# Two-layer attention trunk: softmax weights as the stationary operand of the value matmuls of B, C and D

## The chip, the cores and the metric

One core of a Trainium2 chip runs the whole program. The metric is the device time of one execution in microseconds (us). The kernel before takes 2915.13 us, the median of three runs (2912.08 to 2920.03). In the profile, PE is TensorE's matmuls, PEld its weight loads, DVE VectorE, ACT ScalarE, POOL GpSimd and SP the engine that issues the DMAs.

## The reference

The input x is 2048 rows of 1024 values. Two layers, each with a residual:

```
z = rms_norm(x, ln_g) @ w_in                  # even layer: A and B; odd layer: C and D
q, k = rms_norm(q), rms_norm(k)               # per head of 64
s = q k^T / 8 + bias, masked;  p = softmax(s) # A: two softmaxes, w = p0 - lambda p1
o = p @ v                                     # heads of 64 (A: v of 128, o normed again)
x = x + concat(o * silu(gate)) @ w_out
```

B has 8 heads and sees all earlier rows, its bias is a cumulated forget gate. C has 8 query and 2 key/value heads in a window of two blocks of 128 rows, with a sink per head in the softmax's sum. D has 8 heads and sees up to five blocks, with a bias table by distance.

## The kernel before, in words

Everything runs in blocks of 128 rows (16 of them). Numbers are carried as f32r, a form of f32 that TensorE rounds; a factor that must not lose its rest is split into a high part h (f32r) and a low part l = value - h. The profile prints f32r as f32 in TensorE's rows.

The program is a list of steps, one per block and unit: 4 units of A (64 steps), 4 of B, 16 steps of output projection, 2 units of C, 4 of D, 16 steps of projection. Each step has pieces of four kinds: p (projection: 24 matmuls of 512 columns, `proj`, L214 to L216, then evacuation, norms, gate in `post`), t (transposes of q and k, L248), q (scores, L303, then a fused bias and running minimum on DVE, L306, and the exponential with its sum on ACT, L322) and v (weights times values). `drive` (L815) merges p of step i+2, q of step i and v of step i-1 by cost numbers that stand beside each piece; a scheduler behind it then places every instruction on its engine's in-order queue. A step's x (loads) runs up to four steps ahead.

The v piece of B, C and D is `pairs_av` (L332). It works on pairs of heads. A group of up to four weight tiles of 128 x 128 is transposed on TensorE (`ptp`, L344) into one PSUM bank, copied by ACT to h and by DVE to l (`ptb`, f32r, h and l side by side). Each tile is then one matmul (L365): V is the stationary operand, with its own 64 high and 64 low columns side by side, and h and l together are the moving operand of 256 columns. The result `OT` has head dimensions on its partitions, so it is already transposed; of its four quarters three are wanted, and `end` (L368) adds them with two ACT copies and four DVE operations. The gate is scaled by the softmax's reciprocal sums on DVE, transposed on TensorE (`ptg`, L355) and multiplied in. The product goes to DRAM transposed (`mixT`), and `out_proj` (L673) loads it and splits it on ACT and POOL without a transpose; only A's half of layer 0 is stored as rows (`mix`) and transposed in `out_proj` (`psm`, L689).

A's v (L449) works the other way: the transposed weights are the stationary operand. Per tile it has a matmul of h against V's 128 high and 128 low columns (`OA`, L479) and one of l in bf16 against a bf16 copy of V (L482).

PSUM holds two banks for z, two for scores (`pS`), three for transposes (`pT`) and one for outputs (`pO`).

Of the kernel before, what the change touches and what calls it, by code (L numbers as in the profile page):

```python
# [56 lines left out]
class Trunk:  # L57
    def __init__(self, ctx, tc, t):
# [35 lines left out]
        self.mix = dt_("mix", [P, DM // 2])  # L94
        self.mixT = [dt_("mixTa", [P, DM // 2]), dt_("mixTb", [P, DM])]
# [77 lines left out]
    def transposed(self, xs, dst):  # L173

        nc = self.nc
        for half, x in enumerate(xs):
            ps = self.pT.tile([P, 4, P], F32, tag="t", name="psx")
            for i in range(4):
                nc.tensor.transpose(ps[:, i], x[:, P * i:P * i + P], self.idf[:])  # L179
            xt = self.ap.tile([P, 4, 2, P], F32R, tag="pt", name="xnT", bufs=5)  # L180
            self.split(xt[:, :, 0], xt[:, :, 1], ps[:], nc.scalar, nc.vector)
            nc.sync.dma_start(dst[:, 1024 * half:1024 * half + 1024], xt[:].bitcast(F32).rearrange("p k a t -> p (k a t)"))
# [77 lines left out]
    def v_split(self, z):  # L260
# [5 lines left out]
        return V  # L266

    def silu2(self, z, mul=None):

        nc = self.nc  # L270
        g = self.ap.tile([P, P], F32, tag="gate", name="gate", bufs=8)
# [7 lines left out]
    def qk_row(self, row_st, q, ks, slot, kb0, m, bias, scale, recip):  # L279
# [12 lines left out]
        def piece(i, b, n):  # L292
# [18 lines left out]
            if i == len(cuts) - 1:  # L311
                self.exp_row(row_st, state["prev"], recip)
# [4 lines left out]
    def exp_row(self, row_st, nmax, recip):  # L317
        nc = self.nc
        s = self.sm.tile([P, 2], F32, tag="rs", name="rs")
# [3 lines left out]
        if len(rows) == 2:  # L323
            nc.vector.tensor_tensor(out=s[:, 0:1], in0=s[:, 0:1], in1=s[:, 1:2], op=ALU.add)
        row_st["s"] = s[:, 0:1]
        if recip is not None:
            nc.vector.reciprocal(s[:, 0:1], s[:, 0:1])
            if recip != 1.0:
                nc.gpsimd.tensor_scalar(out=s[:, 0:1], in0=s[:, 0:1], scalar1=recip, scalar2=1.0, op0=ALU.mult, op1=ALU.mult)


    def pairs_av(self, pairs):  # L332
# [3 lines left out]
        groups = [(pr, pr["items"][i:i + 4]) for pr in pairs for i in range(0, len(pr["items"]), 4)]  # L336
        hls = {}

        def tr(gi):
            g = groups[gi][1]  # L340
# [4 lines left out]
            hl = hls[gi] = ap.tile([P, 4, 2, P], F32R, tag="pt", name="ptb", bufs=5)  # L345
            self.split(hl[:, :n, 0, :], hl[:, :n, 1, :], pt[:, :n], nc.scalar, nc.vector)

        def gate(pr):

            g = pr["gate"]()  # L350
            for h in range(2):
                s = slice(64 * h, 64 * h + 64)
                nc.vector.tensor_scalar(out=g[:, s], in0=g[:, s], scalar1=pr["r"][h](), scalar2=0.5, op0=ALU.mult, op1=ALU.mult)
            pt = self.pT.tile([P, P], F32, tag="t", name="ptg")
            nc.tensor.transpose(pt[:], g[:], self.idf[:])  # L355
            gT = pr["gT"] = ap.tile([P, P], F32, tag="gT", name="gT", bufs=2)
            nc.scalar.activation(gT[:], pt[:], AF.Copy)

        def mm(gi):
            pr, g = groups[gi]  # L360
            if "OT" not in pr:
                pool, tag = (self.pO, "o") if pr is pairs[0] else (self.pS, "s")
                pr["OT"] = pool.tile([P, 2, 2, P], F32, tag=tag, name="OT")
            for i, (h, _, V, first, last) in enumerate(g):
                nc.tensor.matmul(pr["OT"][:, h].rearrange("p a b -> p (a b)"), V, hls[gi][:, i].rearrange("p a b -> p (a b)"),  # L365
                                 start=first, stop=last, skip_group_check=True)

        def end(pr):  # L368
            OT = pr["OT"]
            o = ap.tile([P, P], F32, tag="oT", name="oT", bufs=1)  # L370
            top, bot = slice(0, 64), slice(64, 128)
            nc.scalar.activation(o[top], OT[bot, 0, 0], AF.Copy)
            nc.scalar.activation(o[bot], OT[top, 1, 0], AF.Copy)
            nc.vector.tensor_tensor(out=o[top], in0=OT[top, 0, 0], in1=o[top], op=ALU.add)
            nc.vector.tensor_tensor(out=o[bot], in0=OT[bot, 1, 0], in1=o[bot], op=ALU.add)
            nc.vector.tensor_tensor(out=o[top], in0=OT[top, 0, 1], in1=o[top], op=ALU.add)
            nc.vector.tensor_tensor(out=o[bot], in0=OT[top, 1, 1], in1=o[bot], op=ALU.add)
            out = ap.tile([P, P], F32, tag="out", name="out", bufs=2)
            nc.vector.tensor_tensor(out=out[:], in0=o[:], in1=pr["gT"][:], op=ALU.mult)
            nc.sync.dma_start(pr["dst"], out[:])  # L380
        pieces = []
        n = len(groups)
        for gi in range(n + 1):
            if gi < n:
                pieces.append((0.107 * len(groups[gi][1]), lambda gi=gi: tr(gi)))
            if gi:
                pr, g = groups[gi - 1]
                pieces.append((0.107 * len(g), lambda gi=gi: mm(gi - 1)))
                if gi == n or groups[gi][0] is not pr:
                    pieces.append((0.107, lambda pr=pr: gate(pr)))  # L390
                    pieces.append((0.0, lambda pr=pr: end(pr)))
# [8 lines left out]
    def unit_A(self, h, W, X):  # L400
# [4 lines left out]
        def mk(tb):  # L405
# [3 lines left out]
            def p():  # L409
# [8 lines left out]
                def post():  # L418
# [8 lines left out]
                    Vb = self.bp.tile([P, P], BF16, tag="Vb", name="Vb", bufs=18)  # L427
# [14 lines left out]
            def q():  # L442
                st["r"] = [{}, {}]
                out = []
                for c in range(2):
                    out += self.qk_row(st["r"][c], lambda c=c: st["q"][c], ks, c, 0, m, bias, slope, 1.0 if c == 1 else None)
                return out

            def v():  # L449
# [3 lines left out]
                def tr(gi):  # L453
                    r0, r1 = st["r"]
                    j, cm = groups[gi]
                    if gi == 0:
                        cf = st["cf"] = self.sm.tile([P, 1], F32, tag="cf", name="cf")
                        nc.vector.tensor_scalar(out=cf[:], in0=r1["s"], scalar1=r0["s"], scalar2=self.nlam[:, 0:1], op0=ALU.mult, op1=ALU.mult)
# [11 lines left out]
                    l = self.bp.tile([P, 4, P], BF16, tag="ptl", name="ptl", bufs=3)  # L470
# [13 lines left out]
                def end():  # L484
                    O, gate = st["O"], st["gate"]
                    sq = ap.tile([P, P], F32, tag="oT", name="oT", bufs=1)
                    r0 = self.sm.tile([P, 2], F32, tag="r0", name="r0")
                    nc.vector.reciprocal(r0[:, 0:1], st["r"][0]["s"])
                    o = ap.tile([P, P], F32, tag="out", name="out", bufs=2)
                    nc.scalar.activation(o[:], O[:, 0], AF.Copy, scale=r0[:, 0:1])  # L490
                    nc.vector.scalar_tensor_tensor(out=o[:], in0=O[:, 1], scalar=r0[:, 0:1], in1=o[:], op0=ALU.mult, op1=ALU.add)
                    nc.scalar.activation(sq[:], o[:], AF.Square, accum_out=r0[:, 1:2])
                    y = self.rstd(r0[:, 1:2], 1, P, "x")
                    nc.vector.scalar_tensor_tensor(out=o[:], in0=o[:], scalar=y[:, 0:1], in1=gate[:], op0=ALU.mult, op1=ALU.mult)
                    nc.sync.dma_start(self.mix[tb][:, h * P:h * P + P], o[:])
# [12 lines left out]
    def unit_BD(self, kind, u, W, X):  # L508
# [15 lines left out]
        def mk(tb):  # L524
# [35 lines left out]
            def q():  # L560
                st["r"] = [{}, {}]
                out = []
                for h in range(2):
                    out += self.qk_row(st["r"][h], lambda h=h: st["q"][h], ks, h, kb0, m,
                                       lambda b, n, h=h: bias(h, b, n), 1.0, 1.0)
                return out

            def v():
                def w(h, j):
                    return lambda: st["r"][h]["rows"][j // 8][0][:, j % 8 * P:j % 8 * P + P]  # L570
                c0 = P * (u if kind == "B" else 4 + u)
                return self.pairs_av([dict(
                    items=[(h, w(h, j), vs[kb0 + j][:, h], j == 0, j == m - 1) for h in range(2) for j in range(m)],
                    r=[lambda h=h: st["r"][h]["s"] for h in range(2)], gate=lambda: st["gate"], dst=self.mixT[layer][tb][:, c0:c0 + P])])
# [18 lines left out]
    def unit_C(self, kv, W, Wkv, KV, X):  # L593
# [4 lines left out]
        def mk(tb):  # L598
# [6 lines left out]
            def p():  # L605
# [16 lines left out]
                def post():  # L622
# [3 lines left out]
                    st["gate"] = [self.silu2(z[:, 256 + P * i:384 + P * i]) for i in range(2)]  # L626
# [35 lines left out]
            def v():  # L662
                def w(g, j):
                    return lambda: st["row"][:, g, j * P:j * P + P]
                return self.pairs_av([dict(
                    items=[(h, w(2 * i + h, j), vs[kb0 + j][:, kv], j == 0, j == m - 1) for h in range(2) for j in range(m)],
                    r=[lambda g=2 * i + h: st["st"][:, g, 1:2] for h in range(2)], gate=lambda i=i: st["gate"][i],
                    dst=self.mixT[1][tb][:, (2 * kv + i) * P:(2 * kv + i + 1) * P]) for i in range(2)])
# [4 lines left out]
    def out_proj(self, layer, W, hook, done):  # L673
        nc = self.nc

        def mk(tb):
            st = {}

            def x():
# [4 lines left out]
                if layer == 0:  # L684
                    nc.sync.dma_start(mf[:, :512], self.mix[tb][:])
                    nc.sync.dma_start(mf[:, 512:], self.mixT[0][tb][:])
                    ps = self.pT.tile([P, 4, P], F32, tag="t", name="psm")
                    for i in range(4):
                        nc.tensor.transpose(ps[:, i], m[:, i], self.idf[:])  # L689
                else:  # L690
                    nc.sync.dma_start(mf, self.mixT[1][tb][:])
                for half, (h, l, _) in enumerate(st["x"]):
                    if layer == 0 and half == 0:
                        self.split(h, l, ps[:], nc.scalar, nc.vector)
                    else:
# [381 lines left out]
```

## Time and profile before

| | |
|---|---|
| median of three runs | 2915.13 us (2912.08 to 2920.03) |
| profiled execution | 2917.31 us |
| its span, first to last instruction | 2915.5 us |
| TensorE's mean granted clock | 0.989 of full speed |
| busy: PE, PEld | 2819.3, 2383.4 us |
| busy: DVE, ACT, POOL | 2187.9, 1920.4, 1249.3 us |
| A, to the end of its value matmuls | 60 to 815 us (the start takes 60) |
| B | 815 to 1587 us |
| first projection, C, D, last projection | to 1820, 2160, 2740, 2916 us |

Stages overlap at their borders, since the projection of the next unit runs beside the values of the last. Matmuls are pipelined: a matmul's duration in the profile contains latency that overlaps with its neighbours, so the distance between starts tells what it costs, and busy time does not. A weight load (PEld) of the next matmul runs beside the current one. "Idle before" in a group's row is the engine's idle time just ahead of its instructions, with what ended it.

### The profile page before, as it was taken

The page shows a single profiled execution, that of the slowest core. Times are in us where ns is not written, and L with a number is a line of the kernel's source. Part 1 is how long each engine was busy: PE and PEld are TensorE (multiplying, and loading weights), DVE is VectorE, ACT ScalarE, POOL GpSimd, SP SyncE. Part 2 cuts the span into 40 slices and gives each one's busy share as a digit, 9 for nine tenths or more (in the row PEclk, how much of TensorE's full clock was granted, in tenths as well). Part 3 has the DMA queues.
Part 4 walks back from the last instruction along what each step waited for, and adds up shares of the span by engine and source line. Part 5 has one row for each costly group of instructions (what it writes and reads, how often), then busy time and mean ns, then how long its engine had stood idle before and what let it go on. Part 6 is the DMA issues. An engine that isn't in the chain of part 4 may idle for free. (4 is left out here: it accounts for less than half of the span.)

```text
span 2915.5 us, 51639 instructions
## 1 busy us (share of the span) xinstructions
PE 2819.3 (97%) x16256; PEld 2383.4 (82%) x16256; DVE 2187.9 (75%) x7388; ACT 1920.4 (66%) x5127; POOL 1249.3 (43%) x1900
## 2 busy tenths in 40 slices
PE   7999999999999999999999999999999999999999
PEld 5778778787788888888878887988888888888887
DVE  6898887888888788788787334888987778777611
ACT  6567767677677677776776225878877776767510
POOL 5776565655644334333341113343233434343421
PEclk8999999999999999999999999999999999999999
DMA  8433433333333433423324555234443434343442
GB/s 293 157 129 128 134 121 123 107 111 110 115 103 100 131 100 103 143 90 128 116 67 154 216 195 181 98 115 147 137 145 124 154 127 145 126 156 116 148 152 94
DMA packets 159889, 389.30 MB, mean 134 GB/s; under 512 B 18144, under 2 KB 51936, under 8 KB 159616
## 3 DMA queue, kind: packets, MB, share of 16 engines
q1 hardware_dynamic: 159616, 386.00, 39.6%
q8 instruction: 130, 2.13, 0.3%
q14 instruction: 143, 1.17, 0.1%
HBM read 318.75 MB, written 67.17 MB: 132 GB/s over the span
## 5 line engine op out<-in xcount | busy, mean ns | idle before, releaser
L214 PE MATMUL z<-wh,x 128*128 128x512 f32 x1792 | 740.3, 414 | 20.0 <-DVE x L106 13.6
L216 PE MATMUL z<-wh,x 128*128 128x512 f32 x1792 | 715.8, 400 | 4.4 <-POOL x L108 3.6
L215 PE MATMUL z<-wl,x 128*128 128x512 f32 x1792 | 717.3, 400 | 0.8 <-DVE wl L154 0.8
L322 ACT ACTIVATE row<-row,mx 128x1024 f32<-128x1024 f32 (+7 forms) x512 | 440.8, 862 | 191.3 <-DVE mx L306 187.4
L303 PE MATMUL pss<-kT,qT 128*128 128x512 f32 (+3 forms) x1728 | 489.8, 369 | 27.7 <-DVE mx L306 26.1
L214 PEld LDWEIGHTS z<-wh,x 128*128 128x128 f32 x1792 | 342.1, 191 | 76.3 <-ACT wh L153 9.9
L216 PEld LDWEIGHTS z<-wh,x 128*128 128x128 f32 x1792 | 341.1, 190 | 74.3 <-POOL x L108 5.4
L215 PEld LDWEIGHTS z<-wl,x 128*128 128x128 f32 x1792 | 342.7, 191 | 53.3 <-DVE wl L154 3.1
L303 PEld LDWEIGHTS pss<-kT,qT 128*128 128x128 f32 x1728 | 295.2, 190 | 80.4 <-DVE mx L306 40.8
L108 DVE TENSOR_TENSOR ptb<-ptp,ptb 128x512 fp32r<-128x512 f32 (+1 forms) x520 | 326.9, 636 | 20.5 <-ACT ptb L104 16.6
L104 ACT ACTIVATE ptb<-ptp 128x512 fp32r<-128x512 f32 (+1 forms) x520 | 278.2, 554 | 79.9 <-PE ptp L344 73.5
L365 PE MATMUL OT<-ptb,V 128*128 128x256 f32 x1896 | 314.7, 292 | 12.3 <-DVE ptb L108 11.8
L365 PEld LDWEIGHTS OT<-ptb,V 128*128 128x128 f32 x1896 | 273.4, 191 | 43.9 <-DVE ptb L108 20.9
L116 POOL TENSOR_TENSOR y<-v,mhalf 128x4 f32<-128x4 f32 (+2 forms) x326 | 293.3, 901 | 19.7
L108 POOL TENSOR_TENSOR hl<-zs,hl 128x256 fp32r<-128x256 f32 (+1 forms) x240 | 174.0, 725 | 248.4 <-DVE hl L106 170.9
L344 PE MATMUL ptp<-idf,row 128*128 128x128 f32 x1648 | 258.3, 274 | 6.5 <-DVE ptb L108 5.2
L344 PEld LDWEIGHTS ptp<-idf,row 128*128 128x128 f32 x1648 | 198.2, 141 | 37.3 <-DVE ptb L108 4.0
L222 ACT ACTIVATE zs<-z,rs 128x512 f32<-128x512 f32 (+1 forms) x240 | 159.8, 667 | 88.2 <-PE z L216 83.3
L108 POOL TENSOR_TENSOR V<-zs,V 128x128 fp32r<-128x128 f32 x144 | 67.3, 469 | 274.4 <-ACT V L104 274.3
L108 POOL TENSOR_TENSOR wl<-wraw,wh 128x512 fp32r<-128x512 f32 x118 | 154.0, 1311 | 40.6 <-ACT wh L104 34.0
L714 DVE TENSOR_TENSOR res<-zo,res 128x512 f32<-128x512 f32 x64 | 44.0, 689 | 168.2 <-PE zo L216 166.8
L108 POOL TENSOR_TENSOR x<-mixr,x 128x512 fp32r<-128x512 f32 x48 | 62.1, 1296 | 249.8 <-ACT x L104 239.4
(186 smaller groups left out, 6069.3 us busy)
## 6 DMA issues: line engine op xcount, KB each, us to landing
x<-xs SPq DMA_DIRECT2D x416, 512.0 KB, 3.6
wraw<-in_w_dram SPq DMA_DIRECT2D x64, 256.0 KB, 2.8
xs<-x SPq DMA_DIRECT2D x32, 512.0 KB, 4.3
xs<-xnT SPq DMA_DIRECT2D x32, 512.0 KB, 3.3
xraw<-in_xT_dram SPq DMA_DIRECT2D x32, 256.0 KB, 4.2
x<-in_x_dram SPq DMA_DIRECT2D x32, 256.0 KB, 5.8
biasB<-cumd SPq DMA_DIRECT2D x32, 256.0 KB, 3.9
wraw<-in_wo_dram SPq DMA_DIRECT2D x32, 256.0 KB, 2.6
```

The source lines that it names most:

```text
L104: nc.scalar.activation(hi, src, AF.Copy)
L108: lo_eng.tensor_tensor(out=lo, in0=src, in1=h, op=ALU.subtract)
L116: nc.gpsimd.tensor_tensor(out=y[:], in0=v[:], in1=self.mhalf[:, :n], op=ALU.pow)
L214: nc.tensor.matmul(ps(), xh[:, i, :], wh, start=(kb == 0), stop=False)
L215: nc.tensor.matmul(ps(), xh[:, i, :], wl, start=False, stop=False)
L216: nc.tensor.matmul(ps(), xl[:, i, :], wh, start=False, stop=(kb == KB - 1))
L222: self.nc.scalar.activation(zs[:, :n], z[:, :n], AF.Copy, scale=self.rs[layer][:, tb:tb + 1])
L303: nc.tensor.matmul(ps[:, :w], q()[:, j, :], k[:, slot, (b % 4) * P:(b % 4) * P + w], start=(j == 0), stop=(j == 1))
L322: nc.scalar.activation(row[:, :hm * P], row[:, :hm * P], AF.Exp, scale=-1.0, bias=nmax, accum_out=s[:, i:i + 1])
L344: nc.tensor.transpose(pt[:, i], it[1](), self.idf[:])
L365: nc.tensor.matmul(pr["OT"][:, h].rearrange("p a b -> p (a b)"), V, hls[gi][:, i].rearrange("p a b -> p (a b)"), start=first, stop=last, s ...
L714: nc.vector.tensor_tensor(out=o[:, s], in0=st[n][:], in1=o[:, s], op=ALU.add)
```

## The change

`pairs_av` becomes `heads_av`. For B, C and D the transposed weights are now the stationary operand, as in A: per tile one matmul of h (f32r) against V's 64 high and 64 low columns (128 columns), and one of l (now bf16) against a bf16 copy of V's head (64 columns). The result has rows on its partitions; ACT and DVE add its two halves, DVE multiplies by the reciprocal sums and by the gate, for two heads at once in B and D and four in C. The gate isn't transposed any more. Rows go to DRAM as f32 in `mix`, and `out_proj` transposes all eight tiles of a block on TensorE, in both layers, and splits them on ACT and DVE. `v_split` makes the bf16 copy of V on ACT. In A and in the softmax's sums, sums and reciprocals of two rows are joined into one operation (`two_sums`, `add_sums`); `pt` tiles are half as large, with five `ptl` tiles (A had three), two `oT` tiles and an own pair of `xnT` tiles. The cost numbers of the v pieces change with it.

```
@@ v_split
-        return V
+        Vb = self.kvp.tile([P, 2, 64], BF16, tag="Vb", name="Vb", bufs=19)
+        nc.scalar.activation(Vb[:].rearrange("p h d -> p (h d)"), z, AF.Copy)
+        return V, Vb
...
+    def add_sums(self, st):
+        s = st["s"]
+        if len(st["r"][0]["rows"]) == 2:
+            self.nc.vector.tensor_tensor(out=s[:, :, 0], in0=s[:, :, 0], in1=s[:, :, 1], op=ALU.add)
...
-    def pairs_av(self, pairs):
+    def heads_av(self, nh, items, r, gate, dst):
...
-            hl = hls[gi] = ap.tile([P, 4, 2, P], F32R, tag="pt", name="ptb", bufs=5)
-            self.split(hl[:, :n, 0, :], hl[:, :n, 1, :], pt[:, :n], nc.scalar, nc.vector)
-
-        def gate(pr):
-
-            g = pr["gate"]()
-            for h in range(2):
-                s = slice(64 * h, 64 * h + 64)
-                nc.vector.tensor_scalar(out=g[:, s], in0=g[:, s], scalar1=pr["r"][h](), scalar2=0.5, op0=ALU.mult, op1=ALU.mult)
-            pt = self.pT.tile([P, P], F32, tag="t", name="ptg")
-            nc.tensor.transpose(pt[:], g[:], self.idf[:])
...
+            h = ap.tile([P, 4, P], F32R, tag="pt", name="pth", bufs=5)
+            l = ap.tile([P, 4, P], BF16, tag="ptl", name="ptl", bufs=5)
+            hls[gi] = h, l
+            self.split(h[:, :n], l[:, :n], pt[:, :n], nc.scalar, nc.vector)
 
         def mm(gi):
...
-            for i, (h, _, V, first, last) in enumerate(g):
-                nc.tensor.matmul(pr["OT"][:, h].rearrange("p a b -> p (a b)"), V, hls[gi][:, i].rearrange("p a b -> p (a b)"),
-                                 start=first, stop=last, skip_group_check=True)
...
+            for head in sorted({it[0] for _, it in g}):
+                own = [(i, it) for i, it in g if it[0] == head]
+                for i, (_, _, V, first, last) in own:
+                    nc.tensor.matmul(O[:, head], h[:, i], V[0], start=first, stop=False, skip_group_check=True)
+                for i, (_, _, V, first, last) in own:
+                    nc.tensor.matmul(O[:, head, 0:64], l[:, i], V[1], start=False, stop=last, skip_group_check=True)
+
+        def end():
+            O = st["O"]
+            o = ap.tile([P, nh, 64], F32, tag="oT", name="oT", bufs=2)
+            nc.scalar.activation(o[:], O[:, :, 64:128], AF.Copy, scale=0.5)
+            nc.vector.scalar_tensor_tensor(out=o[:], in0=O[:, :, 0:64], scalar=0.5, in1=o[:], op0=ALU.mult, op1=ALU.add)
+            nc.vector.tensor_tensor(out=o[:], in0=o[:], in1=r().unsqueeze(2).broadcast_to([P, nh, 64]), op=ALU.mult)
+            out = ap.tile([P, nh * 64], F32, tag="out", name="out", bufs=2)
+            nc.vector.tensor_tensor(out=out[:], in0=o[:].rearrange("p h d -> p (h d)"), in1=gate()[:], op=ALU.mult)
+            nc.sync.dma_start(dst, out[:])
...
-                pieces.append((0.107 * len(g), lambda gi=gi: mm(gi - 1)))
+                pieces.append((0.095 * len(groups[gi - 1]), lambda gi=gi: mm(gi - 1)))
...
@@ out_proj
-                if layer == 0:
-                    nc.sync.dma_start(mf[:, :512], self.mix[tb][:])
-                    nc.sync.dma_start(mf[:, 512:], self.mixT[0][tb][:])
+                nc.sync.dma_start(mf, self.mix[layer][tb][:])
+                for half, (h, l, _) in enumerate(st["x"]):
                     ps = self.pT.tile([P, 4, P], F32, tag="t", name="psm")
                     for i in range(4):
-                        nc.tensor.transpose(ps[:, i], m[:, i], self.idf[:])
...
-                        self.split(h, l, m[:, 4 * half:4 * half + 4], nc.scalar, nc.gpsimd)
+                        nc.tensor.transpose(ps[:, i], m[:, 4 * half + i], self.idf[:])
+                    self.split(h, l, ps[:], nc.scalar, nc.vector)
```

What this makes of the order shows at three places. The first is TensorE's queue in unit B, at a group of four weight tiles of one head; before (`row` holds the weights, `V` the values of one block, z is the projection of a later step):

```order
L215 MATMUL z_15592<-wl_11409,x_15258 128x512
L216 MATMUL z_15592<-wh_11408,x_15258 128x512
L344 MATMUL ptp_15301<-idf_87,row_15116 128x128 x4
L365 MATMUL OT_15165<-ptb_15178,V_14384 128x256
L365 MATMUL OT_15165<-ptb_15178,V_14514 128x256
L365 MATMUL OT_15165<-ptb_15178,V_14639 128x256
L365 MATMUL OT_15165<-ptb_15178,V_14769 128x256
```

and in the changed kernel, where `pth` is h and `ptl` is l (line numbers have shifted, so L213 to L215 are `proj` here):

```order
L214 MATMUL z_16967<-wl_14437,x_16469 128x512
L367 MATMUL OT_16545<-V_14530,pth_16603 128x128
L367 MATMUL OT_16545<-V_14651,pth_16603 128x128
L367 MATMUL OT_16545<-V_14786,pth_16603 128x128
L367 MATMUL OT_16545<-V_14929,pth_16603 128x128
L215 MATMUL z_16967<-wh_14436,x_16469 128x512
L213 MATMUL z_16967<-wh_14550,x_16469 128x512
L369 LDWEIGHTS ptl_16604
L369 MATMUL OT_16545<-Vb_14533,ptl_16604 128x64
```

Four matmuls became four with h and, here after two matmuls of a later projection, four with l, of which the first stands in the last two rows; each of them changes the stationary operand.

The second is DVE's queue in B, where a pair of heads ends; before:

```order
L374 TENSOR_TENSOR oT_21981<-OT_21861,oT_21981 64x128
L375 TENSOR_TENSOR oT_21981<-OT_21861,oT_21981 64x128
L106 CAST hl_22181<-zs_22159 128x4x64
L108 TENSOR_TENSOR ptb_22054<-ptp_22049,ptb_22054 128x4x128
L306 ISA row_22063,mx_22062<-pss_22083,biasB_20289,mx_22062 128x512
L306 ISA mx_22062 128x1
L376 TENSOR_TENSOR oT_21981<-OT_21861,oT_21981 64x128
L377 TENSOR_TENSOR oT_21981<-OT_21861,oT_21981 64x128
```

and in the changed kernel:

```order
L375 SCALAR_TENSOR_TENSOR oT_21454<-OT_21364,oT_21454 128x128
L376 TENSOR_TENSOR oT_21454<-oT_21454,rs_20978 128x128
L107 TENSOR_TENSOR ptl_21523<-ptp_21517,pth_21522 128x512
L378 TENSOR_TENSOR out_21458<-oT_21454,gate_20953 128x128
L308 ISA row_21496,mx_21470<-pss_21497,db_21500,mx_21470 128x128
```

Four additions of half tiles, spread over other work, became one of a whole tile, with two multiplications behind it.

The third is TensorE's queue in the last projection, at the border of two blocks (`zo` is the projection's PSUM tile, `mixr` the loaded rows); before:

```order
L214 MATMUL zo_39860<-wk_38813,x_39707 128x512
L215 MATMUL zo_39860<-wk_38813,x_39707 128x512
L216 MATMUL zo_39860<-wk_38813,x_39707 128x512
L214 MATMUL zo_39889<-wh_36789,x_39769 128x512
L215 MATMUL zo_39889<-wl_36790,x_39769 128x512
```

and in the changed kernel:

```order
L213 MATMUL zo_40106<-wk_39032,x_39915 128x512
L214 MATMUL zo_40106<-wk_39032,x_39915 128x512
L215 MATMUL zo_40106<-wk_39032,x_39915 128x512
L694 MATMUL psm_40137<-idf_87,mixr_40135 128x128 x4
L213 MATMUL zo_40153<-wh_36966,x_39987 128x512
```

Four transposes of a later block's rows stand between the matmuls, in a queue that held none of them in this layer.

More of the change, by code (lines that the diff above doesn't have):

```diff
@@ L368, in end @@
[L368 to L380, printed above, removed]
+            h = ap.tile([P, 4, P], F32R, tag="pt", name="pth", bufs=5)
@@ L625, in post @@
                     next(g)
-                    st["gate"] = [self.silu2(z[:, 256 + P * i:384 + P * i]) for i in range(2)]
+                    st["gate"] = self.silu2(z[:, 256:512])
                     next(g)
```

110 lines of the change are left out of this document (53 added, 57 removed).

## The prediction

> **What bounds the kernel now.** I read the page's busy shares first, then the stages (windows), then what TensorE waits for, and last its timeline, because a pipelined engine's busy time does not show what one of its instructions costs.
>
> ```profile
> span 2915.5 us, 51639 instructions
> PE 2819.3 (97%) x16256; PEld 2383.4 (82%) x16256; DVE 2187.9 (75%) x7388; ACT 1920.4 (66%) x5127; POOL 1249.3 (43%) x1900
> ```
>
> ```profile
> 60.00:815.00 755.00, 720.76 (x4258) 587.82 (x4258) 646.16 (x2047) 508.99 (x1360) 474.60 (x701) 0.99 0.37 123
> 815.00:1587.00 772.00, 757.30 (x4586) 653.00 (x4584) 638.83 (x2151) 563.79 (x1377) 289.36 (x477) 1.00 0.34 110
> 1587.00:1820.00 233.00, 228.11 (x1145) 189.83 (x1144) 91.44 (x247) 83.71 (x202) 51.19 (x83) 0.97 0.56 202
> 1820.00:2160.00 340.00, 328.54 (x2024) 287.55 (x2023) 290.07 (x1139) 281.19 (x888) 128.92 (x198) 0.98 0.40 129
> 2160.00:2740.00 580.00, 572.38 (x3330) 494.03 (x3329) 454.99 (x1630) 416.67 (x1140) 236.03 (x358) 0.99 0.41 134
> 2740.00:2916.00 176.00, 170.40 (x768) 140.77 (x766) 31.56 (x61) 24.30 (x48) 38.74 (x30) 1.00 0.38 134
> ```
>
> The six rows are A, B, the first output projection, C, D and the last projection; after the colon pair stand the length and the busy time of PE, PEld, DVE, ACT and POOL, then clock and DMA. TensorE is idle for 772.0 - 757.3 = 14.7 us in B, 11.5 in C and 7.6 in D, together 34 us of 1692, and for 34 us in A. DVE is at 83%, 85% and 78% in B, C and D. So TensorE sets the time in all the stages that change, and what remains idle there mostly waits for DVE:
>
> ```profile
> L365 PE MATMUL OT<-ptb,V 128*128 128x256 f32 x1896 | 314.7, 292 | 12.3 <-DVE ptb L108 11.8
> PE pss L303 <- DVE mx L306: 26.1, 39, 1.8
> ```
>
> The busy time of a row of matmuls overlaps with its neighbours', so costs have to come from start to start. One stretch of B, and the same stretch's weight loads (PEld):
>
> ```profile
> 1003.38 0.40 PE L216 MATMUL z<-wh,x 128*128 128x512 f32 x1
> 1003.61 0.63 PE L365 MATMUL OT<-ptb,V 128*128 128x256 f32 x4
> 1004.09 0.60 PE L344 MATMUL ptp<-idf,row 128*128 128x128 f32 x4
> ```
>
> ```profile
> 1003.99 0.46 PEld L344 LDWEIGHTS ptp<-idf,row 128*128 128x128 f32 x4
> 1004.41 0.54 PEld L365 LDWEIGHTS OT<-ptb,V 128*128 128x128 f32 x4
> ```
>
> A 512-column f32r matmul takes 1003.61 - 1003.38 = 0.23 us, a value matmul of 256 columns (1004.09 - 1003.61)/4 = 0.12 (its loads, 0.19 long by the mean below, start (0.54 - 0.19)/3 = 0.117 apart; I use 0.119). So 256 columns cost 0.11, and a 128-column f32r matmul would stream for about 0.12 - 0.055 = 0.065 us if columns alone counted. They do not:
>
> ```profile
> 1940.37 0.97 PEld L646 LDWEIGHTS psC<-kT,qT 128*128 128x128 f32 x8
> 1940.40 1.08 PE L646 MATMUL psC<-kT,qT 128*128 128x128 f32 x8
> 1941.32 0.62 PE L344 MATMUL ptp<-idf,rowC 128*128 128x128 f32 x4
> ```
>
> These eight matmuls of C's scores have an f32r operand of 128 columns and a new f32r stationary operand each, the form the change brings in. They take (1941.32 - 1940.40)/8 = 0.115 us apiece, not 0.065. The loads show why: one lasts 0.19 (its mean below), so eight in 0.97 start (0.97 - 0.19)/7 = 0.111 apart. The loads run one after the other; a matmul shorter than 0.111 us waits for the next load, a 256-column one (0.12) just hides it.
>
> **The change part by part.** *Value matmuls.* Removed: 1896 matmuls of 256 columns at 0.119: 225.6 us, their loads hidden. Added: 1896 matmuls h of 128 f32r columns and 1896 matmuls l of 64 bf16 columns, each with its own load. For l the nearest rows are A's bf16 matmuls of 128 columns:
>
> ```profile
> 511.40 0.40 PE L482 MATMUL OA<-Vb,ptl 128*128 128x128 bf16 x4
> 511.61 0.72 PE L479 MATMUL OA<-VA,pth 128*128 128x256 f32 x4
> ```
>
> ```profile
> L365 PEld LDWEIGHTS OT<-ptb,V 128*128 128x128 f32 x1896 | 273.4, 191 | 43.9 <-DVE ptb L108 20.9 <-ACT ptb L104 0.8 <-issue 0.7
> L344 PEld LDWEIGHTS ptp<-idf,row 128*128 128x128 f32 x1648 | 198.2, 141 | 37.3 <-DVE ptb L108 4.0 <-issue 3.7 <-PE pss L303 1.4
> L482 PEld LDWEIGHTS <-ptl 128*128 128x128 bf16 x544 | 31.7, 98 | 29.6 <-issue 9.8 <-DVE ptl L108 6.5 <-DVE mx L306 2.9
> ```
>
> Four take 511.61 - 511.40 = 0.21, or 0.052 each, for 128 columns. An f32r load of 191 ns occupies 111, so 80 of a load's duration is latency; then a bf16 load (98) occupies 18 ns and that of a transpose (141) 61. With 64 columns l lies between its load, 18 ns, and the 128-column row, 52; I take half the stream and a few ns, 30.
>
> What a load costs depends on the matmul ahead of it, so I counted neighbours in the built order of TensorE. Of the matmuls with f32r weights, 1362 stand behind an h (1193 of them h) and 515 behind an l (369 of them h); 186 transposes stand behind an l. The sum in us: streams 1896 x 0.065 = 123.2 and 1896 x 0.030 = 56.9; loads sticking out behind an h 1362 x (0.111 - 0.065) = 62.7, behind an l 515 x (0.111 - 0.030) = 41.7; transposes behind an l 186 x (0.061 - 0.030) = 5.8. Total 290.3, against 225.6: **+65 us**. Bounds: l at 18 or 52 ns moves only the 1195 l that follow an l, by -14 or +26; were h's own stream as long as its load, the 477 l and few others behind an h would add some 25. So +50 to +115.
>
> The Trainium skill, "TensorE: Matmul & The Clock Gate", section "Back-to-back issue gap", gives 81 ns per matmul in a stream of loads and matmuls of 128 columns; by it the 3792 new ones would take an estimated 307 us, +81, the same sign.
>
> *Transposes.* The 192 gate transposes go and 192 of mixed rows come (4 more per block of 128 rows in the first projection, 8 in the last), one kind of instruction at one price, by the loads of the stretch above (0.46 - 0.14)/3 = 0.107 each: 0 on TensorE in all, 21 us moved out of B, C and D, into the projections. There they stand in TensorE's queue behind a load from DRAM, with the projection's matmuls behind them:
>
> ```profile
> L689 PE MATMUL psm<-idf,mixr 128*128 128x128 f32 x64 | 9.6, 273 | 0.2 <-DMA mixr<-mix 0.2
> ```
>
> The 64 that exist waited 0.2 us for it in all, so I put this wait at nothing; the cover is the four steps by which the load is issued ahead.
>
> *VectorE and ScalarE.* The seven small DVE operations of an output pair go:
>
> ```profile
> L353 DVE TENSOR_SCALAR gate<-gate,rs 128x64 f32<-128x64 f32 x256 | 86.9, 340 | 4.6
> L353 DVE TENSOR_SCALAR gate<-gate,stC 128x64 f32<-128x64 f32 x128 | 31.2, 297 | 0.5
> L374 DVE TENSOR_TENSOR oT<-OT,oT 64x128 f32<-64x128 f32 x192 | 53.6, 279 | 37.5 <-ACT oT L373 33.1 <-PE pss L303 1.5
> L375 DVE TENSOR_TENSOR oT<-OT,oT 64x128 f32<-64x128 f32 x192 | 56.6, 295 | 6.0
> L376 DVE TENSOR_TENSOR oT<-OT,oT 64x128 f32<-64x128 f32 x192 | 53.8, 280 | 3.5
> L377 DVE TENSOR_TENSOR oT<-OT,oT 64x128 f32<-64x128 f32 x192 | 54.6, 284 | 6.0
> L379 DVE TENSOR_TENSOR out<-oT,gT 128x128 f32<-128x128 f32 x192 | 64.5, 336 | 1.5
> L491 DVE SCALAR_TENSOR_TENSOR out<-OA,r,out 128x128 f32<-128x128 f32 x64 | 21.9, 342 | 0.8 <-ACT out L490 0.8
> L108 DVE TENSOR_TENSOR x<-psm,x 128x512 fp32r<-128x512 f32 x16 | 11.0, 689 | 30.4 <-ACT x L104 30.4
> ```
>
> That is 401 us. In come three operations per step: for B and D 128 x (342 + 336 + 336), for C 32 times the same at twice the width (about 480 each by these rows), and 48 splits of 689 in the projections, where DVE idles: 130 + 46 + 33. VectorE loses about 190 us, 225 in B, C and D less 33 in the projections, and a few more by joined sums and reciprocals (in A too). ScalarE loses three operations per pair and gains an evacuation and a bf16 copy of V (297 ns by A's rows); neither it nor POOL, which loses 48 splits, bounds a stage.
>
> What can TensorE get back? At least nothing: a lighter VectorE adds no speed to a load. At most all its idle time, 34 us in B, C and D and 34 in A. I take two thirds of the first, 22, since DVE sheds a sixth of its 1384 us in B, C and D and its two waits above are the main ones, and 6 in A, where little goes: **-28**.
>
> *Sum.* The profiled execution took 2917.3 us, its span 2915.5 and 1.8 around it. 2917.3 + 65 - 28 = 2954; the median of the runs, 2915.1, lies 2.2 below the profiled one, so 2952.
>
> **The rivals.** *1. Loads of f32r weights do hide behind 128 columns* (faster). Then h costs 0.065 and l 0.030 wherever they stand: 180 against 225.6, -45, with the relief -73: 2842. It decides from a load below 65 ns. Against it stand psC's eight loads 111 ns apart; for it only that those are scores, not weighted values. The Trainium skill, same page, section "Weight-path perf modes", says that the fast weight load is on with 128 weights and an input that is not FP32; were f32r counted so, this is what would happen. By this trace it is not: 191 ns for an f32r load, 98 for a bf16 one.
>
> *2. The relief takes it all back.* VectorE's late work shows not only as idle time but as loads issued too late (20.9 us of waits in L365's loads above). If these went as well, some 60 us return: 2917 + 65 - 62 = 2920, no change, a little faster at the lower bound of the loads. For it: DVE's 83%. Against it: TensorE's 97%, and A keeps half of the idle time.
>
> *3. The projections stall.* The 32 blocks' transposes now wait for rows from DRAM in TensorE's queue; at 2 us a block 64 us: 3016. The 0.2 us above is against it.
>
> **How the numbers follow.** Forecast 0.70 (2924 to 2992), rival 1 0.10, rival 2 0.14, rival 3 or a cost above the bounds 0.06. The range, 2912 to 2992, leaves out rival 1 and the faster end of rival 2 below, rival 3 above. About 0.3% is what a measurement can tell from no change, 2906 to 2924. Faster: rival 1 and a third of rival 2, 0.14; same: the rest of rival 2, 0.10; slower: 0.76.
>
> **What would show it.** In the changed kernel's timeline four h should start 0.11 us apart and their loads too, and l about 0.03; h at 0.065 would be rival 1. PE's idle time in B, C and D should fall from 34 us to some 12 while these stages still grow; DVE's total should be near 2000 or a little less. Waits of psm for mixr above 10 us would be rival 3. If B grows by less than 15 us with h at 0.11, rival 2 holds.

## The result, and the profile after

The changed kernel takes 2952.08 us, the median of four runs (2950.8 to 2953.78), beside 2916.35 for the kernel before on the same chip: a ratio of 1.0123, 95% interval 1.0106 to 1.0141. It is slower by 36 us; the forecast was 2952.

The page's first lines, of the profiled execution of the changed kernel:

```profile
span 2951.9 us, 53646 instructions
PE 2876.8 (97%) x18152; PEld 2435.1 (82%) x18152; DVE 1981.1 (67%) x6282; ACT 1834.3 (62%) x4821; POOL 1188.0 (40%) x1852
```

VectorE lost 207 us, ScalarE 86 and POOL 61, and still the span is 36 us longer; TensorE's share is 97% as before. Where the time came from shows when both spans are cut at the same places, the first projection matmul of each unit (A, B, first output projection, C, D, last projection; columns as in the prediction's windows). Before:

```profile
0.00:735.00 735.00, 687.70 (x3958) 557.30 (x3959) 615.11 (x1953) 497.66 (x1344) 455.48 (x685) 0.98 0.42 141
735.00:1536.00 801.00, 782.53 (x4741) 671.46 (x4740) 666.42 (x2260) 583.94 (x1441) 327.91 (x537) 1.00 0.33 109
1536.00:1761.00 225.00, 223.62 (x1159) 187.45 (x1158) 100.45 (x242) 87.07 (x189) 39.09 (x55) 1.00 0.54 193
1761.00:2106.00 345.00, 331.12 (x2022) 288.87 (x2021) 272.56 (x1069) 266.47 (x829) 125.87 (x202) 0.97 0.40 130
2106.00:2725.00 619.00, 608.91 (x3531) 524.55 (x3531) 490.68 (x1779) 450.86 (x1257) 253.75 (x388) 0.99 0.42 136
2725.00:2916.00 191.00, 185.40 (x856) 153.77 (x854) 42.69 (x92) 34.41 (x71) 47.18 (x37) 1.00 0.39 135
```

and after:

```profile
0.00:728.00 728.00, 683.50 (x3952) 554.54 (x3953) 601.71 (x1862) 495.26 (x1340) 453.79 (x681) 0.98 0.42 142
728.00:1542.00 814.00, 803.94 (x5683) 689.99 (x5682) 597.80 (x1920) 562.65 (x1387) 329.26 (x539) 1.00 0.33 108
1542.00:1774.00 232.00, 231.83 (x1309) 195.48 (x1309) 101.98 (x242) 84.39 (x183) 18.44 (x39) 1.00 0.53 187
1774.00:2119.00 345.00, 339.10 (x2225) 297.49 (x2224) 221.59 (x780) 243.37 (x711) 125.49 (x200) 0.97 0.39 130
2119.00:2750.00 631.00, 620.76 (x4007) 533.30 (x4006) 405.06 (x1388) 419.74 (x1149) 254.51 (x390) 0.99 0.40 134
2750.00:2952.00 202.00, 197.65 (x986) 164.28 (x984) 52.96 (x95) 28.91 (x55) 6.53 (x6) 1.00 0.35 128
```

A is 7 us shorter, B 13 longer, the first projection 7, C even, D 12, the last projection 11. TensorE's idle time in B, C and D fell from 18 + 14 + 10 = 42 to 10 + 6 + 10 = 26 us. So B and D, which have new value matmuls, grew although TensorE rests less in them; in C its rest shrank by as much as its work grew. The projections, which were given the transposes, grew too.

A stretch of B in the timeline after, PE first and then its weight loads:

```profile
1202.51 0.29 PE L369 MATMUL OT<-Vb,ptl 128*128 128x64 bf16 x4
1202.63 0.64 PE L367 MATMUL OT<-V,pth 128*128 128x128 f32 x4
1203.12 0.29 PE L369 MATMUL OT<-Vb,ptl 128*128 128x64 bf16 x4
```

```profile
1202.61 0.53 PEld L367 LDWEIGHTS OT<-V,pth 128*128 128x128 f32 x4
1203.11 0.17 PEld L369 LDWEIGHTS <-ptl 128*128 128x128 bf16 x4
```

Four l take 1202.63 - 1202.51 = 0.12 us, 0.030 each. Four h take 0.49, and their loads, 0.19 long each, start (0.53 - 0.19)/3 = 0.113 apart: half the columns of before for nearly the same 0.12.

### The profile page after: what moved, and what is told of

Same layout as the page of the kernel before. It is cut to its first block, busy times and chain, and to the rows that moved or that the text cites. A ratio compares the mean times of both kernels' runs of the same rounds, so it can differ in the third digit from the quotient of the medians.

```text
span 2951.9 us, 53646 instructions
## 1 busy us (share of the span) xinstructions
PE 2876.8 (97%) x18152; PEld 2435.1 (82%) x18152; DVE 1981.1 (67%) x6282; ACT 1834.3 (62%) x4821; POOL 1188.0 (40%) x1852
## 4 chain that ended last, share of the span: by engine, by line
PE 74%; DVE 11%; POOL 5%; ACT 4%; issue 3%; DMA 3%; SPq 0%; POOLq 0%; DVEq 0%; ACTq 0%
PE z L213 11%; PE z L214 11%; PE z L215 11%; PE pss L305 8%; PE ptp L352 7%; PE OT L367 6%; PE zo L213 4%; PE zo L215 4%; PE zo L214 4%; DVE row L308 3%; PE OT L369 2%; PE ptq L247 2%; POOL y L115 1%; DVE ptl L107 1%; DVE row L467 1%
## 5 line engine op out<-in xcount | busy, mean ns | idle before, releaser
L213 PE MATMUL z<-wh,x 128*128 128x512 f32 x1792 | 729.4, 408 | 16.8 <-DVE x L105 12.9
L215 PE MATMUL z<-wh,x 128*128 128x512 f32 x1792 | 717.3, 401 | 4.4 <-POOL x L107 3.6
L305 PE MATMUL pss<-kT,qT 128*128 128x512 f32 (+3 forms) x1728 | 501.3, 373 | 20.3 <-DVE mx L308 18.5
L213 PEld LDWEIGHTS z<-wh,x 128*128 128x128 f32 x1792 | 342.0, 191 | 76.4 <-ACT wh L152 10.3
L215 PEld LDWEIGHTS z<-wh,x 128*128 128x128 f32 x1792 | 341.2, 190 | 71.1 <-POOL x L107 5.7
L107 DVE TENSOR_TENSOR ptl<-ptp,pth 128x512 bf16<-128x512 f32 (+1 forms) x518 | 326.2, 640 | 77.1 <-ACT pth L103 74.6
L103 ACT ACTIVATE pth<-ptp 128x512 fp32r<-128x512 f32 (+1 forms) x518 | 276.0, 556 | 123.0 <-PE ptp L352 120.0
L367 PE MATMUL OT<-V,pth 128*128 128x128 f32 x1896 | 314.0, 278 | 0.1
L367 PEld LDWEIGHTS OT<-V,pth 128*128 128x128 f32 x1896 | 281.9, 193 | 14.6 <-ACT pth L103 0.6
L352 PEld LDWEIGHTS ptp<-idf,row 128*128 128x128 f32 x1648 | 191.2, 142 | 22.5 <-PE pss L305 1.0
L369 PE MATMUL OT<-Vb,ptl 128*128 128x64 bf16 x1896 | 177.2, 198 | 1.5 <-DVE ptl L107 1.5
L117 DVE TENSOR_TENSOR q<-y 128x4 f32<-128x4 f32 (+2 forms) x326 | 85.6, 263 | 126.5 <-POOL y L115 124.8
```

The lines of the kernel that those rows point to most:

```text
L103: nc.scalar.activation(hi, src, AF.Copy)
L107: lo_eng.tensor_tensor(out=lo, in0=src, in1=h, op=ALU.subtract)
L213: nc.tensor.matmul(ps(), xh[:, i, :], wh, start=(kb == 0), stop=False)
L215: nc.tensor.matmul(ps(), xl[:, i, :], wh, start=False, stop=(kb == KB - 1))
L305: nc.tensor.matmul(ps[:, :w], q()[:, j, :], k[:, slot, (b % 4) * P:(b % 4) * P + w], start=(j == 0), stop=(j == 1))
L352: nc.tensor.transpose(pt[:, i], it[1](), self.idf[:])
```

## The experiments

Each line of the table is a median, and its ratio to the kernel before on the same chip; the changed kernel itself stands first. The last column is the mean clock granted to TensorE in the run's one profiled execution. The kernel before took 2916.4 to 2917.8 us beside them.

| run | us | ratio (95%) | clock |
|---|---|---|---|
| changed kernel | 2952.1 | 1.0123 (1.0106 to 1.0141) | 0.988 |
| e1_bf16_h | 2850.6 | 0.9768 (0.9752 to 0.9783) | 0.990 |
| e2_alternate | 2994.0 | 1.0263 (1.0248 to 1.0278) | 0.991 |
| e3_wide_h | 2973.3 | 1.0193 (1.0178 to 1.0208) | 0.992 |
| e7_no_l | 2859.1 | 0.9800 (0.9785 to 0.9816) | 0.988 |
| f1_bf16_all | 2842.0 | 0.9745 (0.9728 to 0.9763) | 0.990 |
| e4_light_end | 2888.0 | 0.9906 (0.9890 to 0.9923) | 0.994 |
| e5_dve_back | 2944.6 | 1.0093 (1.0075 to 1.0111) | 0.993 |
| e8_no_scale | 2906.6 | 0.9959 (0.9945 to 0.9972) | 0.992 |
| e9_one_add | 2883.5 | 0.9887 (0.9874 to 0.9901) | 0.992 |
| e10_hold_bank | 2940.0 | 1.0080 (1.0066 to 1.0093) | 0.994 |
| e11_behind | 2902.5 | 0.9946 (0.9932 to 0.9959) | 0.990 |
| e12_bank | 2898.2 | 0.9937 (0.9925 to 0.9950) | 0.991 |

### What the loads cost: five runs on the first term

**e1_bf16_h**, the load taken away and nearly all else kept:

```
@@ heads_av
-            h = ap.tile([P, 4, P], F32R, tag="pt", name="pth", bufs=5)
+            h = ap.tile([P, 4, P], BF16, tag="pt", name="pth", bufs=5)
@@ v_split
-        V = self.kvp.tile([P, 2, P], F32R, tag="V", name="V", bufs=19)
+        V = self.kvp.tile([P, 2, P], BF16, tag="V", name="Vb", bufs=19)
...
-        Vb = self.kvp.tile([P, 2, 64], BF16, tag="Vb", name="Vb", bufs=19)
-        nc.scalar.activation(Vb[:].rearrange("p h d -> p (h d)"), z, AF.Copy)
-        return V, Vb
+        return V, V4[:, :, 0]
```

> The changed kernel with h in bf16 and V in B, C and D split into bf16 high and low parts, so that every value matmul has a bf16 load (the products keep 16 bits or so instead of f32r's). Theory (f32r loads behind short matmuls are the cost): a load of 98 ns length instead of 191 occupies about 18 ns and hides; h 0.055, l 0.030 us each, with what still sticks out 186 us of TensorE instead of 290: -104, some of it lost because VectorE comes nearer to being the bound: 2848 to 2880 us, h starts 0.055 us apart. Rival (columns alone count, loads hide anyway): h goes from 0.065 to 0.055, -19 us: about 2933.

Measured 2850.6: 101 us less than the changed kernel. Its timeline of B:

```profile
1204.24 0.39 PE L365 MATMUL OT<-Vb,pth 128*128 128x128 bf16 x4
1204.47 0.28 PE L367 MATMUL OT<-Vb,ptl 128*128 128x64 bf16 x4
```

```profile
1204.21 0.24 PEld L365 LDWEIGHTS <-pth 128*128 128x128 bf16 x4
```

An h now starts every (1204.47 - 1204.24)/4 = 0.058 us, and its four loads are done in 0.24 us where those of the changed kernel take 0.53. The number of columns and of VectorE's operations is that of the changed kernel, and the order of the matmuls nearly so: it is not the same instruction for instruction, but 1200 h stand behind an h in this trace and 1193 in that of the changed kernel. The type of the operands, and with it the load, is not. ScalarE also loses the copy of V, 32 us of its busy time. The rival that lets columns alone count gave 2933.

**e2_alternate**, h and l of each tile in turn:

```
                 for i, (_, _, V, first, last) in own:
                     nc.tensor.matmul(O[:, head], h[:, i], V[0], start=first, stop=False, skip_group_check=True)
-                for i, (_, _, V, first, last) in own:
                     nc.tensor.matmul(O[:, head, 0:64], l[:, i], V[1], start=False, stop=last, skip_group_check=True)
```

> The changed kernel with h and l of each tile in turn instead of all h of a group and then all l. Theory (one load ahead only, so it starts when the matmul before starts): 1583 h instead of 369 stand behind an l of 0.030 us and stick out by 0.081, none behind an h: value matmuls 332 us instead of 290, +42: 2985 to 3000. Rival (loads can run several matmuls ahead, so that only their sum of 0.111 + 0.018 per tile counts): 245 us, -45: about 2907.

Measured 2994.0, +42: the same instructions in another order cost as much as the neighbours' sum said. Two l of that kernel, one pair apart, and its weight loads:

```profile
1207.53 0.20 PE L368 MATMUL OT<-Vb,ptl 128*128 128x64 bf16 x1
1207.72 0.20 PE L368 MATMUL OT<-Vb,ptl 128*128 128x64 bf16 x1
```

```profile
1207.54 0.20 PEld L367 LDWEIGHTS OT<-V,pth 128*128 128x128 f32 x1
1207.71 0.10 PEld L368 LDWEIGHTS <-ptl 128*128 128x128 bf16 x1
1207.72 0.20 PEld L367 LDWEIGHTS OT<-V,pth 128*128 128x128 f32 x1
```

A pair takes 0.19 us by its matmuls and 1207.72 - 1207.54 = 0.18 by its loads, near the 0.065 + 0.111 = 0.176 of one load ahead and far from the 0.129 of several; the short load of l starts 0.17 behind the long one of h. That the total fits to the microsecond is in part chance: over the whole trace a pair takes 0.187, which makes 17 us more for the 1583, while the profiled execution has 8 us less idle time of TensorE than that of the changed kernel (67 against 75) and about 9 us less missing clock (0.991 against 0.988).

**e3_wide_h**, twice the columns where the load already sets the pace:

```
-                st["O"] = self.pO.tile([P, nh, P], F32, tag="o", name="OT")
+                st["O"] = self.pO.tile([P, nh, 4 * P // nh], F32, tag="o", name="OT")
...
-                    nc.tensor.matmul(O[:, head], h[:, i], V[0], start=first, stop=False, skip_group_check=True)
+                    nc.tensor.matmul(O[:, head].rearrange("p (a d) -> p a d", d=P), h[:, i], V[0].unsqueeze(1).broadcast_to([P, 4 // nh, P]),
+                                     start=first, stop=False, skip_group_check=True)
```

> The changed kernel with the h matmuls of B and D widened to 256 columns (V's 128 columns twice, the second half unused); C keeps 128. Theory (load-bound): 1648 streams grow by 0.054 us, +89, but about 1180 loads behind an h, 0.046 each, disappear, -54: +35, 2980 to 2995, h 0.119 us apart. Rival (columns alone count): +89, about 3040.

Measured 2973.3, +21: 14 less than the theory's sum and 68 less than by columns alone. Its h:

```profile
1206.94 0.64 PE L367 MATMUL OT<-V,pth 128*128 128x256 f32 x4
1207.42 0.39 PE L215 MATMUL z<-wh,x 128*128 128x512 f32 x1
```

(1207.42 - 1206.94)/4 = 0.12, against 0.11 with half the columns. The missing 14 us lie outside the matmuls as far as the two profiled executions tell: PE's busy time grew by 21 us (2876.8 to 2898.1) with about 12 us less missing clock in it (0.992 against 0.988, see the end), so by some 33 of the 35 expected at full clock, and its idle time fell by 3.

**e7_no_l**, without the line of the l matmuls (h's last matmul closes the group instead):

> The changed kernel without the l matmuls (the weights' low part is left out of the values; the split that makes it stays). Theory: the 1896 l cost their streams, 57 us, and the f32r loads that stick out behind them; with h alone the value matmuls take 123 us of streams and 1723 loads behind an h at 0.046, 202 instead of 290: -88, 2860 to 2870. Rival (an l costs its 0.030 us only): -57, about 2895.

Measured 2859.1, -93, 5 more than expected: an l costs 0.049 us, of which 0.030 is its start to start. The rest is, by the theory, the next f32r load, which an l is too short to hide.

**f1_bf16_all**, e1 with A done like the rest; of its edit, A's V:

```
-                    V = self.kvp.tile([P, 2, P], F32R, tag="V", name="VA", bufs=19)
+                    V = self.kvp.tile([P, 2, P], BF16, tag="V", name="VA", bufs=19)
...
-                    Vb = self.kvp.tile([P, P], BF16, tag="Vb", name="Vb", bufs=19)
-                    nc.scalar.activation(Vb[:], z[:, 256:384], AF.Copy)
-                    vs.append((V, Vb))
+                    vs.append((V, V[:, 0]))
```

> The kernel with h in bf16 (expected and measured above at 2851) with A done in the same way: V in bf16 high and low parts, h in bf16, no further copy of V. Theory: A's 544 h matmuls stream for 0.109 instead of 0.119 us, and their loads no longer stick out behind an l: 10 us of TensorE less, 2836 to 2845. Rival (A is bound by VectorE, at 86% there, and gains nothing): 2847 to 2853.

Measured 2842.0, 9 us less than e1, within what was expected. It is 2.6% faster than the kernel before and 3.7% faster than the changed one.

### Where the relief came from: seven runs on the second term

**e4_light_end**, the kernel before with the change's relief alone:

```
-            for h in range(2):
-                s = slice(64 * h, 64 * h + 64)
-                nc.vector.tensor_scalar(out=g[:, s], in0=g[:, s], scalar1=pr["r"][h](), scalar2=0.5, op0=ALU.mult, op1=ALU.mult)
...
-            nc.vector.tensor_tensor(out=o[top], in0=OT[top, 0, 0], in1=o[top], op=ALU.add)
-            nc.vector.tensor_tensor(out=o[bot], in0=OT[bot, 1, 0], in1=o[bot], op=ALU.add)
-            nc.vector.tensor_tensor(out=o[top], in0=OT[top, 0, 1], in1=o[top], op=ALU.add)
-            nc.vector.tensor_tensor(out=o[bot], in0=OT[top, 1, 1], in1=o[bot], op=ALU.add)
+            nc.vector.tensor_tensor(out=o[:], in0=OT[:, 0, 0], in1=o[:], op=ALU.add)
```

> The kernel before with a lighter end of B, C and D and nothing else changed: the gate isn't scaled by the reciprocal sums, and one addition of a whole tile stands for the four of half tiles (so the output leaves out that scaling and adds a wrong quarter). VectorE loses about 270 us, as much as or a little more than by the change. Theory (the relief is real, 28 us of the sum): 2880 to 2900 us. Rival (TensorE gets nothing back and the loads cost 36 us alone): 2910 to 2918.

Measured 2888.0: -29 against the 28 of the sum, with 225 us less on VectorE (2187.9 to 1963.3). The size fits; the next run asked whether the reason does.

**e5_dve_back**, the changed kernel with part of VectorE's work given back:

```
+            for _ in range(4):
                 nc.vector.tensor_tensor(out=out[:], in0=o[:].rearrange("p h d -> p (h d)"), in1=gate()[:], op=ALU.mult)
```

> The changed kernel with VectorE's saving given back: the last multiplication of each output (by the gate) is done four times instead of once, 480 more operations of 336 to 480 ns, some 190 us. Theory (a lighter VectorE gave TensorE about 28 us): 2970 to 2980 us. Rival (the gain came from fewer waits between ScalarE, VectorE and the one output bank, or from the sums joined in A, not from VectorE's total): under 2958.

Measured 2944.6, not slower but 7 us faster, although VectorE is busier by 122 us:

```profile
PE 2867.5 (98%) x18152; PEld 2428.4 (83%) x18152; DVE 2103.1 (72%) x6762; ACT 1833.6 (62%) x4821; POOL 1192.9 (41%) x1852
```

The 122 us are part of the 207 that VectorE lost, and by the theory they would cost some 16 us; TensorE's idle time (span less PE) even fell, from 75 to 69 us. So the theory that VectorE's total gave the relief falls for this kernel. Two others were set against it: the one output bank is held for less time, or the form of the operations counts.

**e8_no_scale** takes only the first block out of e4's diff, **e9_one_add** only the second:

> The kernel before without the two VectorE operations that scale a gate by the reciprocal sums (left out of the output), 118 us of VectorE; the reading of the output bank is as before. Theory D (what TensorE got back is VectorE's total): 118 of the 270 us that gave 28, so -12: 2904. Theory B (it is the time that the one output bank is held, until the additions of an output are done): no change, 2913 to 2919.

> The kernel before with one addition of a whole tile in place of the four of half tiles (a wrong quarter is added), some 150 us of VectorE less; the gate is scaled as before. Theory B (the output bank): about -28, as with both: 2888 to 2893. Theory D (VectorE's total): 150 of 270, -16: 2901.

Measured 2906.6 (-10) and 2883.5 (-33). By itself e8 lies nearer to theory D (VectorE's busy time fell by 84 us there, not 118), and e9 beyond what either gave. They do not add up: with both blocks out, e4 gained 29, less than e9 alone. So the additions carry the relief, and the scaling is worth 10 us without them and nothing on top of them. The clock does not explain the 10: its mean over the five runs is 0.992 and over the nine of the kernel before beside them 0.991, some 2 us.

**e10_hold_bank** repeats in the changed kernel the operation that reads the bank:

```
+            out = ap.tile([P, nh * 64], F32, tag="out", name="out", bufs=2)
+            for _ in range(3):
+                nc.vector.scalar_tensor_tensor(out=out[:].rearrange("p (h d) -> p h d", d=64), in0=O[:, :, 0:64], scalar=0.5, in1=o[:], op0=ALU.mult, op1=ALU.add)
             nc.vector.scalar_tensor_tensor(out=o[:], in0=O[:, :, 0:64], scalar=0.5, in1=o[:], op0=ALU.mult, op1=ALU.add)
```

> The changed kernel with the reading of the output bank by VectorE done four times instead of once (three results are overwritten), so that the bank is held about 1.1 us longer per output and VectorE has 480 more operations. Theory B: most of the 28 us is given back, 2970 to 2980. Theory D says the same for a total given back, but the earlier run with the extra work behind the bank came out at 2945, so without B: 2940 to 2955.

Measured 2940.0: holding the bank longer costs the changed kernel nothing that can be seen. For the kernel before, the prediction's row of L365 says much the same: its matmuls, which write the bank, waited 12.3 us in all, 11.8 of them for the weights' low part, which leaves 0.5 for the bank. The last two runs go back to e9 and bring its VectorE work up again, behind the bank or on it (shown against e9):

```
@@ e11_behind
+            for _ in range(4):
                 nc.vector.tensor_tensor(out=out[:], in0=o[:], in1=pr["gT"][:], op=ALU.mult)
@@ e12_bank
+            for _ in range(3):
+                nc.vector.tensor_tensor(out=out[:], in0=OT[:, 0, 0], in1=o[:], op=ALU.add)
             nc.vector.tensor_tensor(out=o[:], in0=OT[:, 0, 0], in1=o[:], op=ALU.add)
```

> The kernel before with one addition (as in e9_one_add, whose low quarter it leaves out too) and the last multiplication of each pair done four times: VectorE has as many operations and as much time per pair as before the change, but the output bank is free after one addition. If the half-tile additions cost by holding the bank: stays at 2880 to 2890. If they cost by VectorE's time at that place: back to 2905 to 2917.

> The kernel before with one addition that is done four times from the output bank (three results are overwritten, the low quarter is left out as in e9_one_add): four additions again, of whole tiles and with the bank held as long as before. If holding the bank or VectorE's time costs: back to 2905 to 2917. If only the half-tile form costs (two of them work on other partitions than they write): stays at 2880 to 2890.

Measured 2902.5 and 2898.2: both between the two answers, and alike. With the bank free early or held late it is the same, so holding the bank is not what costs. VectorE's time at that place brings back 15 to 19 of the 33 us, in the kernel before; the other half goes with the half-tile form (of the four additions one, L377, reads other partitions than it writes, not two), or with the order that the scheduler gives each of these programs, which no run separates. That stays open. TensorE's idle time, 96 us in the kernel before, is 94 in e8, 82 in e9, 84 in e4, 90 in e11 and 87 in e12, so idle time is less than half of what e9 gained.

## Why the prediction was right

**What bounds.** TensorE's share stayed at 97% while VectorE, ScalarE and POOL lost 354 us together. Right.

**+65 for the value matmuls.** The h at 0.11 and l at 0.03 are in the timeline, and four runs moved this term and little else: -101 (-104 expected), +42 (+42, in part by chance), -93 (-88) and +21 (+35). The mechanism is right; the size came out somewhat smaller, as the next but one paragraph says. The rows that carried it were not those of the instruction to be replaced but of C's scores, where the kernel before has eight 128-column f32r matmuls in a row, each with a new f32r operand.

**Transposes at 0, moved.** The first projection grew by 7 us and the last by 11; 64 and 128 transposes at 0.107 are 7 and 14. The new waits behind DRAM did not come, so rival 3 is out:

```profile
L694 PE MATMUL psm<-idf,mixr 128*128 128x128 f32 x256 | 37.7, 278 | 0.0
```

**-28 for the relief.** The page shows the two terms side by side: TensorE's busy time grew by 2876.8 - 2819.3 = 57.5 us, not 65, and its idle time (span less PE) fell from 96.2 to 75.1, by 21, not 28. The missing clock of the two profiled executions is nearly the same. So both terms were about 7 us too large, and that their sum hits to the microsecond is luck. The split is not exact, because a wait that is shorter than a matmul's latency counts as busy. In B, C and D idle time fell by 16 us where 22 were forecast and ended at 26, not at some 12; in A, where 6 were forecast, it fell by 3 (47.3 to 44.5). The reason given, that VectorE sheds a sixth of its work and TensorE gets idle time for it, is not shown: giving 122 us of the work back in the changed kernel cost nothing, and in the kernel before VectorE's time brought back at most about half of the 33 us. Near in size, open in cause.

**Rival 1** is refuted for f32r by the loads 0.113 apart; e1 and f1 show that a time near its 2842 was there to be had with bf16 loads, by another change than the one made. **Rival 2** lost, but a mark set for it was wrong: B grew by only 13 us, under the 15 named, with h at 0.11. The mark looked at one stage; D and the projections hold 30 us of the growth, and the whole came out where the forecast put it. VectorE's busy time, near 2000 or a little less, came out at 1981.

## What to carry to other kernels

In this kernel a matmul costs the longer of its own stream and the next one's weight load, as if only one load ran ahead: with f32r weights 256 columns (0.12 us) just hide a load (0.111 to 0.113) and 128 columns do not, so halving the columns saved next to nothing, and a very short matmul in between made the next load stick out. Before swapping the stationary operand, look in the trace for an instruction of the same operand types and width, wherever it stands, and measure its start to start. If a bf16 pair of high and low parts is exact enough, its load is short enough to hide: the swap that lost 36 us here gains 66 with it (e1), and 75 with A done in the same way.

## What the hardware showed that was not expected

Short waits of TensorE can cost more than their length. In D of the changed kernel TensorE waited 1.94 us for a bias row from DRAM (timeline, then windows over the same place; the clock is the third number from the right):

```profile
2448.26 1.51 PE L593 MATMUL psb<-flip,anti 128*128 128x320 f32 x4 [1.94 <-DMA flip<-in_d_rel_dram]
2449.57 0.42 PE L369 MATMUL OT<-Vb,ptl 128*128 128x64 bf16 x4
```

```profile
2449.00:2456.00 7.00, 7.00 (x36) 5.73 (x34) 4.04 (x15) 2.89 (x7) 1.18 (x2) 0.52 0.17 63
2439.00:2449.00 10.00, 8.06 (x47) 6.82 (x46) 7.50 (x23) 7.32 (x22) 7.39 (x11) 1.00 0.72 256
```

For the next 7 us the granted clock was 0.52, with TensorE busy all the time: 3.4 us of work lost behind a wait of 1.9. "TensorE: Matmul & The Clock Gate" of the Trainium skill tells of a gate with two settings, half and full, that falls after an idle window of some 3.4 us (Part 1, "What's actually happening"); the halves agree, but here a pause of 1.9 us was enough.

Not every such pause does it. In B of the same execution a wait of 1.86 us left the clock of the next 7 us at 1.00:

```profile
1115.31 0.73 PE L305 MATMUL pss<-kT,qT 128*128 128x512 f32 x2 [1.86 <-DVE mx L308]
```

```profile
1116.00:1123.00 7.00, 7.00 (x44) 6.05 (x43) 3.95 (x16) 3.34 (x8) 3.14 (x5) 1.00 0.37 123
```

The fourteen traces tell the two apart. Their records of the clock change only on a fixed beat of 3.41 us, and behind the start of the program it is the idle time of TensorE within one beat that goes with the next: after a beat at full clock with 1.9 us or more of it the clock was half each time, after one with less than 1.1 never, and in between sometimes. The wait of 1.94 us lay within one beat, that of 1.86 was cut by a border into 1.2 and 0.7.

These stretches are not the same in each program, nor in each run of one (0.988 to 0.991 in the four of the changed kernel), and they blur small differences. The mean clock of two profiled executions:

```profile
core 0: 2951.9 us, clock 0.988
```

```profile
core 0: 2939.5 us, clock 0.994
```

The first is the changed kernel, the second e10_hold_bank. Missing clock is 0.012 x 2952 = 35 us in the one and 0.006 x 2940 = 18 in the other: 17 us, more than the 12 between their times. Over the four runs of each the difference is smaller: the mean clock is 0.990 for the changed kernel, 0.991 for e5 and 0.993 for e10, which makes 30, 26 and 20 us of missing clock. So 10 of the 12 us that e10 gained and 4 of the 7 of e5 go with the clock, and without it the work given back cost nothing that can be seen.

The relief in the kernel before is for the most part not clock. The mean over all runs is 0.991 for the kernel before, 0.992 for e4 and 0.993 for e9: some 1 to 2 us of e4's 29 and 4 of e9's 33.
